# One hybrid decoder layer: another order of the projection blocks, the last y in SBUF, and a second top-k by lookups of two-byte values

## The chip, the cores and the metric

The kernel runs on one core of a Trainium2 chip. The metric is the device time of one execution in microseconds (us). The engines are named as the profile names them: PE (matrix multiplication), PEld (its weight loads), DVE (vector), ACT (activations), POOL (issues gathers and the transfers that accumulate), SP (issues the other transfers). Each runs its own instructions in a fixed order and waits on semaphores for the others.

## The reference

One layer on 512 tokens of width 1024, with 16 learned meta tokens put in front, all in fp32. It has two residual sub-layers and a last RMSNorm:

```
u = rmsnorm(h);  z, xBC, dt, conf = split(u @ w_in)
xBC  = silu(causal depthwise conv of width 4)
y    = chunked scan (chunks of 128, 16 heads, 4 groups), + D * x, * silu(z), rmsnorm per group
hc   = causal depthwise conv of width 31 of a * sigmoid(g)     (a, g = conf)
c    = silu(LayerNorm(hc))
h    = h + concat(y, c) @ w_out

q    = rmsnorm(h) @ w_query                    # 8 heads, two halves
v1,i1 = top16(q1 . keys1);  v2,i2 = top16(q2 . keys2)          # of 128 each
top_s, pos = top16(v1[:, None] + v2[None, :])                  # of 256 sums
expert = i1 * 128 + i2 at pos;  gate = softmax(top_s)
h    = h + sum_k gate_k * gelu(x . w_down[expert_k]) * w_up[expert_k]
out  = rmsnorm(h) without the meta tokens
```

There are 16384 experts, each one row of w_down and one of w_up.

## The kernel before, in words

An fp32 product is made of three matmuls of rounded halves (mm3, L160 to L162): high by high, high by low, low by high. A weight block is loaded raw by SP, rounded by ACT (L181, L182), and its low half is finished by a transfer of POOL that accumulates (L183). Two raw and two split buffers alternate.

Stage 1 (0 to 39 us) normalizes the tokens in five tiles (four of 128 and the 16 meta tokens), transposes them (L280) and splits them into halves (L263, L264). z0, the first projection block, is multiplied after that, tile by tile of tokens, with its split weights (L207) loaded in two halves.

Stage 2 (to about 310 us) runs the other 19 blocks of 96 matmuls. The string ORDER names them: z blocks are the gates of y, x blocks the inputs of the scan with their short convolution (taps L362 to L373 on DVE), c blocks the Conformer's. A c block (L398 on) leaves a and g in PSUM; DVE multiplies them (L406, L407: the GLU) and then makes 30 taps of 128x512 on DVE (L413), with late priority (LOWP). The first c block's sum over its channels is used as an offset for the others (L419, L393). When x4 to x7 and a group's own x and z blocks are done, the group's scan follows (ssd, L505 on): per chunk matmuls, exponentials on ACT, and on DVE L515 to L544. It writes y to DRAM (yD). PSUM has two rings of four tiles, pa and pb.

Stage 3 (to 488 us): y is read back, transposed (L591) and split (L597, L598). The output projection has four blocks of four weight rows (out_part), each with two column halves and its own adds into the residual (L620). The Conformer's LayerNorm takes sums over all channels by matmuls with ones (L643, L644), in PSUM columns that each get two matmuls; the moments are L646 to L653. Its results are transposed rows (L393 again), then L658 to L663. Blocks 0 and 1 belong to y, 2 and 3 to the Conformer. The second RMSNorm follows (L669 to L682, transposes L581).

Stage 4 (488 to 600 us): queries, keys, and the first top-16 of 128 for 4 token tiles, 8 heads and 2 halves (L743 to L747, at L789's scores).

Stage 5 (600 to 1026 us): the second top-16 per token tile, in the order 3, 0, 1, 2 (second, L826 on). Only the pairs that can be among the best 16 sums are built, 50 per head, with their sums (cS) and their expert numbers (cI); the expert number at each of the 16 places is picked by a compare with 50 numbers, a product and a sum over 3200 fp32 elements, for each half of the heads (L836, L838, L839). For tiles 0 to 2 both indices and the gate are transposed (L858) and kept as two-byte values. They become dense gate maps (L916 to L938, 12 of 32 tokens), while PE runs 88 blocks of x @ w_down of 24 matmuls each (down). Tile 3 is done by gathering rows: POOL issues each gather (L873), DVE uses it (L889, L896), through two buffers at first.

Stage 6 (from 1026 us) runs the 128 up blocks with what is left of down and of the gathers, and the last norm.

A scheduler that models the engines sets each engine's order, by priorities and offsets: early(SSDP) for the scan, late(LOWP) for the taps, early(YP) with YP = -500 for the output of y, early(LNP) for the LayerNorm.

Of the kernel before, what the change touches and what calls it, by code (L numbers as in the profile page):

```python
# [43 lines left out]
ORDER = "z0 x4 x5 x6 x7 x0 c0 c1 x1 c2 x2 c3 z1 x3 c4 c5 z2 c6 z3 c7".split()  # L44
# [73 lines left out]
def body(ctx, tc, I, out):  # L118
# [146 lines left out]

    for n, t in enumerate(MO):
# [7 lines left out]
        for half in range(2):  # L274
# [7 lines left out]
            split_to(uTh[:, half * 4:half * 4 + 4, c0:c0 + parts], uTl[:, half * 4:half * 4 + 4, c0:c0 + parts], pv)  # L282

# [23 lines left out]
    yD = dram.tile([4, 128, 1024], F32, name="yD")  # L307


    dtraw = con(80)  # L310

    def z_block(k):
        if k == 0:
            zn = 272
            wh, wl = zsplit
        else:
            zn = 256
            wh, wl = next_w()
        for t in MO if k == 0 else range(4):
            p = ps("pa")  # L320
            c0 = NM + 128 * t if t >= 0 else 0
            z0 = 0 if t >= 0 else 256
            for dc in range(8):
                mm3(p[:, z0:zn], uTh[:, dc, c0:c0 + 128], uTl[:, dc, c0:c0 + 128],
                    wh[:, dc * zn + z0:dc * zn + zn], wl[:, dc * zn + z0:dc * zn + zn], dc == 0, dc == 7)
            if k == 0:
                V.tensor_copy(dtraw[:, 16 * (t + 1):16 * (t + 2)], p[:, 256:272])
            if t < 0:
                continue
            zt = ZB[k % 2][:, t, :]  # L330
            S.activation(zt, p[:, :256], AF.Tanh, scale=0.5)
            V.scalar_tensor_tensor(zt, zt, 1.0, p[:, :256], op0=OP.add, op1=OP.mult)
# [169 lines left out]
    def ssd(g):  # L502
# [4 lines left out]
        for c in range(5):  # L507
# [11 lines left out]
            if c > 0:  # L519
# [18 lines left out]
                y_ = ybs[n % 3]  # L538
# [9 lines left out]
                load(yD[c - 1, :, 256 * g:256 * g + 256], y_)  # L548
# [36 lines left out]
    yh = [mem(B0 + 512 * k, 512) for k in range(4)]  # L585
# [22 lines left out]
    def out_part(b):  # L608
        for hf in range(2):
            po = [ps("pa") for _ in range(4)]  # L610
            src = I["wout"][hf, b].rearrange("p k n -> p (k n)")
            wh, wl = wsplit(wload(src), src)
            for t in range(4):
                for k in range(4):
                    sh, sl = hl((b % 2) * 4 + k)
                    mm3(po[t], sh[:, 128 * t:128 * t + 128], sl[:, 128 * t:128 * t + 128],
                        wh[:, 512 * k:512 * k + 512], wl[:, 512 * k:512 * k + 512], k == 0, k == 3)
            for t in range(4):
                hh = h1[t][:, 512 * hf:512 * hf + 512]
                V.tensor_tensor(hh, hh, po[t], op=OP.add)  # L620

    with early(YP):
        n = 0
        for g in range(2):
            for t in range(4):
                load(yq[n % 4], yD[t, :, 256 * g:256 * g + 256])
                y_split(yq[n % 4], t, g, 1)
                n += 1
        for t in range(4):
            load(h1[t], I["x"][128 * t:128 * t + 128])  # L630
        out_part(0)
        for t in range(4):
            load(yh[t], yD[t, :, 512:1024])
            y_split(yh[t], t, 2, 2)
        out_part(1)


    with early(LNP):
        p = ps()
        for c0, (a_, b_) in ((0, (sumd, convo[:, 7, :])), (4, (sumq, sq7[0]))):  # L640
            for t in range(4):
                ts = slice(128 * t, 128 * t + 128)
# [397 lines left out]
```

## Time and profile before

| what | value |
| --- | --- |
| median of three runs | 1749.32 us (1747.53 to 1750.86) |
| profiled execution | 1744.54 us, span 1742.8 us |
| granted clock of PE, mean | 0.969 |
| PE busy | 1642.9 us, 94% |
| DVE busy | 1446.8 us, 83% |
| ACT busy | 767.2 us, 44% |
| POOL busy | 394.3 us, 23% |

Rows of groups read: line, engine, operation, output <- inputs, shapes, count | busy us, mean ns | idle time of the engine just before, and what ended it. Rows of waits read: who <- whom: us in total, times, longest.

### The profile page before, as it was taken

The numbers are of one execution on the slowest core, as the hardware profiler recorded it, in microseconds if no ns is written. First come the engines' busy times: TensorE is split into PE (matmuls) and PEld (weight loads), VectorE is DVE, ScalarE is ACT, GpSimd is POOL, SyncE is SP. The second block draws the span as 40 slices with busy tenths as digits, with TensorE's granted clock in tenths as the row PEclk, the third lists the DMA queues.
The fourth block names the chain that finished last, engine by engine and source line by source line (L and its number), as shares of the span: only waits on it lengthen the run. The fifth ranks groups of instructions, "written<-read, shape, count | busy, mean of one in ns | idle before, by whom it ended". The sixth has DMA issues, their size and how long they took to land.

```text
span 1742.8 us, 26076 instructions
## 1 busy us (share of the span) xinstructions
PE 1642.9 (94%) x9529; PEld 1485.8 (85%) x9529; DVE 1446.8 (83%) x2873; ACT 767.2 (44%) x1117; POOL 394.3 (23%) x317
## 2 busy tenths in 40 slices
PE   6999999758989999989999999999999999999997
PEld 6999899637778899979988988888888899999996
DVE  4559999995359999999888988888888888888885
ACT  5655555434333334424655873333333333333333
POOL 1001011110000002423333003223222255444540
PEclk9999999867999999989999999999999999999999
DMA  6766567443532346768897789999999999999992
GB/s 207 170 156 155 130 153 186 135 117 82 145 106 73 97 159 232 265 211 284 296 310 288 271 290 375 342 347 364 343 341 366 325 322 364 345 351 342 327 333 81
DMA packets 163025, 426.43 MB, mean 245 GB/s; under 512 B 14144, under 2 KB 80960, under 8 KB 154832
## 3 DMA queue, kind: packets, MB, share of 16 engines
q1 hardware_dynamic: 122144, 262.22, 42.9%
q0 software_dynamic: 40752, 162.55, 30.2%
q8 instruction: 74, 1.21, 0.3%
q14 instruction: 55, 0.45, 0.1%
HBM read 382.24 MB, written 42.47 MB: 244 GB/s over the span
## 4 chain that ended last, share of the span: by engine, by line
PE 74%; DMA 10%; DVE 6%; issue 5%; ACT 3%; POOL 2%; SPq 0%; POOLq 0%; DVEq 0%; ACTq 0%
PE pa L162 16%; PE pa L161 16%; PE pa L160 16%; PE pb L162 6%; PE pb L160 6%; PE pb L161 6%; DMA MR<-win 3%; DVE M L413 3%; DMA M<-wu,M 3%; POOL M L873 1%; DMA MR<-wout 1%; PE pb L932 1%; PE pb L933 1%; DMA M<-wd,M 1%; PE pb L786 1%
## 5 line engine op out<-in xcount | busy, mean ns | idle before, releaser
L161 PE MATMUL pa<-MR 128*128 128x512 f32 (+3 forms) x2120 | 729.0, 344 | 5.1 <-DMA MR<-wout 5.1
L160 PE MATMUL pa<-MR 128*128 128x512 f32 (+3 forms) x2120 | 728.8, 345 | 5.3 <-ACT M L761 2.5
L162 PE MATMUL pa<-MR 128*128 128x512 f32 (+3 forms) x2120 | 690.2, 345 | 10.0 <-DVE MR L739 6.1
L162 PEld LDWEIGHTS pa<-MR 128*128 128x128 f32 x2120 | 402.4, 190 | 43.1 <-DVE MR L739 6.6
L160 PEld LDWEIGHTS pa<-MR 128*128 128x128 f32 x2120 | 404.1, 191 | 37.4 <-ACT M L761 3.4
L161 PEld LDWEIGHTS pa<-MR 128*128 128x128 f32 x2120 | 403.5, 190 | 36.3 <-DMA MR<-wout 6.3
L738 ACT ACTIVATE MR<-M 128x1024 fp32r<-128x1024 f32 (+1 forms) x264 | 286.0, 1084 | 289.9 <-PE pa L161 122.0
L739 DVE TENSOR_TENSOR MR<-M,MR 128x1024 fp32r<-128x1024 f32 (+1 forms) x264 | 329.3, 1250 | 45.2 <-ACT MR L738 44.3
L873 POOL DMA_INDIRECT M<-wd,M x128 | 171.4, 1339 | 491.5 <-DVE M L889 229.3
L873 POOL DMA_INDIRECT M<-wu,M x128 | 173.6, 1356 | 363.7 <-DVE M L896 215.5
L160 PE MATMUL pb<-MR 128*128 128x384 f32 (+1 forms) x576 | 206.9, 359 | 0.0
L161 PE MATMUL pb<-MR 128*128 128x384 f32 (+1 forms) x576 | 206.6, 359 | 0.0
L162 PE MATMUL pb<-MR 128*128 128x384 f32 (+1 forms) x576 | 205.5, 359 | 0.0
L959 ACT ACTIVATE MR<-M 128x384 fp32r<-128x384 f32 x128 | 66.9, 523 | 264.8 <-issue 208.4
L896 DVE SCALAR_TENSOR_TENSOR M<-M 128x1024 f32<-128x1024 f32 x128 | 163.6, 1278 | 17.9 <-DMA M<-wu,M 17.6
L413 DVE SCALAR_TENSOR_TENSOR M<-M 128x512 f32<-128x512 f32 x240 | 170.6, 740 | 2.4 <-ACT M L411 2.2
L889 DVE SCALAR_TENSOR_TENSOR M<-M 128x1024 f32<-128x1024 f32 x128 | 154.4, 1216 | 6.4 <-DMA M<-wd,M 6.3
L960 DVE TENSOR_TENSOR MR<-M,MR 128x384 fp32r<-128x384 f32 x128 | 71.0, 556 | 59.1 <-ACT MR L959 59.1
L161 PEld LDWEIGHTS pb<-MR 128*128 128x128 f32 x576 | 108.1, 188 | 11.4
L160 PEld LDWEIGHTS pb<-MR 128*128 128x128 f32 x576 | 108.1, 188 | 11.3
L935 ACT ACTIVATE M<-pb 128x512 f32<-128x512 f32 x96 | 97.0, 1159 | 46.2 <-PE pb L933 43.5
L162 PEld LDWEIGHTS pb<-MR 128*128 128x128 f32 x576 | 108.1, 188 | 10.4
(217 smaller groups left out, 1521.4 us busy)
## 6 DMA issues: line engine op xcount, KB each, us to landing
M<-wdT SPq DMA_DIRECT2D x128, 512.0 KB, 5.1
M<-wu SPq DMA_DIRECT2D x128, 512.0 KB, 6.7
GD<-M SPq DMA_DIRECT2D x40, 512.0 KB, 6.2
M<-GD SPq DMA_DIRECT2D x32, 640.0 KB, 7.9
M<-win SPq DMA_DIRECT2D x19, 1024.0 KB, 4.8
MR<-win POOLq DMA_DIRECT2D x19, 1024.0 KB, 8.2
HD<-M SPq DMA_DIRECT2D x88, 192.0 KB, 4.0
M<-HD SPq DMA_DIRECT2D x88, 192.0 KB, 6.2
```

The costliest lines, as they stand in the source:

```text
L160: E.matmul(o, lh, rh, start=first, stop=False)
L161: E.matmul(o, lh, rl, start=False, stop=False)
L162: E.matmul(o, ll, rh, start=False, stop=last)
L413: V.scalar_tensor_tensor(o, gl[:, j:j + 512], cw[:, j:j + 1], o, op0=OP.mult, op1=OP.add)
L738: S.activation(wh, raw, AF.Copy)
L739: leng.tensor_tensor(wl, raw, wh.bitcast(F32), op=OP.subtract)
L873: r = G.indirect_dma_start(out=g, out_offset=None, in_=src, in_offset=bass.IndirectOffsetOnAxis(ap=e3[:, k:k + 1], axis=0))
L889: use(V.scalar_tensor_tensor(g, g, 1.0, x2s, op0=OP.mult, op1=OP.mult, accum_out=dots[:, k:k + 1]))
L896: use(V.scalar_tensor_tensor(h1[3], g, act3[:, k:k + 1], h1[3], op0=OP.mult, op1=OP.add))
L935: S.activation(gb.rearrange("p i t -> p t i")[:, c:c + 4, :], p.rearrange("p (t i) -> p t i", t=4), AF.Copy, scale=1.0 / GS)
L959: S.activation(sh, sf, AF.Copy)
L960: V.tensor_tensor(sl, sf, sh.bitcast(F32), op=OP.subtract)
```

## The change

Five things change.

1. ORDER: c0 comes directly behind z0, c1 behind x4, c2 behind x6; c3, c4 and c5 keep places in the middle, c6 and c7 stay last.
2. z0 is multiplied as each token tile is transposed and split (z_tile); its weights are split at the first tile, and the second half of them is loaded before the meta tokens. The norm weight is loaded before the constants.
3. The y of the last group stays in SBUF (YL) and is neither written to DRAM nor read. Group 2 is read alone. Output blocks 2 and 3 accumulate into one PSUM tile, so that each residual half gets one add less.
4. The LayerNorm's sums are 16 matmuls into 16 columns, and a DVE instruction more adds the halves.
5. The second top-k builds 80 candidates in a grid of 10 rows of 8 (three adds), takes the place of each winner, turns it into a place in each of the two lists of 16, and picks the two indices by a lookup of 16 two-byte values each: compare, product, and four adds that halve the row.

The core of the diff:

```diff
-ORDER = "z0 x4 x5 x6 x7 x0 c0 c1 x1 c2 x2 c3 z1 x3 c4 c5 z2 c6 z3 c7".split()
+ORDER = "z0 c0 x4 c1 x5 x6 c2 x7 x0 z1 x1 c3 c4 z2 x2 c5 z3 x3 c6 c7".split()
...
+    def z_tile(k, t, zn, wh, wl):
+        p = ps("pa")
+        c0 = NM + 128 * t if t >= 0 else 0
+        z0 = 0 if t >= 0 else 256
+        for dc in range(8):
+            mm3(p[:, z0:zn], uTh[:, dc, c0:c0 + 128], uTl[:, dc, c0:c0 + 128],
+                wh[:, dc * zn + z0:dc * zn + zn], wl[:, dc * zn + z0:dc * zn + zn], dc == 0, dc == 7)
...
-        if n == 1:
+        if n == 0:
             z_split()
...
+        z_tile(0, t, 272, *zsplit)
...
-                y_ = ybs[n % 3]
+                y_ = ybs[n % 3] if g < 3 else YL[c - 1]
...
-                load(yD[c - 1, :, 256 * g:256 * g + 256], y_)
+                if g < 3:
+                    load(yD[c - 1, :, 256 * g:256 * g + 256], y_)
...
+            todo = [(t, n) for n in range(len(bs)) for t in range(4)]
+            for t, n in todo if hf == 0 else sorted(todo):
+                wh, wl = ws[n]
+                for k in range(4):
+                    sh, sl = hl((bs[n] % 2) * 4 + k)
+                    mm3(po[t], ..., n == 0 and k == 0, n == len(bs) - 1 and k == 3)
+                if n == len(bs) - 1:
+                    hh = h1[t][:, 512 * hf:512 * hf + 512]
+                    V.tensor_tensor(hh, hh, po[t], op=OP.add)
...
+        out_part([0])
+        y_group(2)
         for t in range(4):
-            load(yh[t], yD[t, :, 512:1024])
-            y_split(yh[t], t, 2, 2)
-        out_part(1)
+            y_split(YL[t], t, 3, 1)
+        out_part([1])
...
-        for c0, (a_, b_) in ((0, (sumd, convo[:, 7, :])), (4, (sumq, sq7[0]))):
+        for c0, src in ((0, sumd), (4, sumq), (8, convo[:, 7, :]), (12, sq7[0])):
             for t in range(4):
-                E.matmul(p[:, c0 + t:c0 + t + 1], a_[:, ts], ones[:, 0:1], start=True, stop=False)
-                E.matmul(p[:, c0 + t:c0 + t + 1], b_[:, ts], ones[:, 0:1], start=False, stop=True)
+                E.matmul(p[:, c0 + t:c0 + t + 1], src[:, 128 * t:128 * t + 128], ones[:, 0:1], start=True, stop=True)
...
-    out_part(2)
-    out_part(3)
+    out_part([2, 3])
...
+    def lookup(o, at, values):
+        half = lambda a: a.rearrange("p n (j s) -> p n j s", s=2)
+        io = iota16[:, 0:16].rearrange("p (j s) -> p j s", s=2)[:, None].to_broadcast([128, 128, 8, 2])
+        V.tensor_tensor(half(oneh), io, at[:, :, None, :].to_broadcast([128, 128, 8, 2]), op=OP.is_equal)
+        h4 = lambda a: a.rearrange("p (h k) c -> p h k c", h=8)
+        V.tensor_tensor(h4(picked), h4(oneh), values[:, :, None, :].to_broadcast([128, 8, 16, 16]), op=OP.mult)
+        src = picked
+        for f in fold:
+            n = f.shape[2]
+            V.tensor_tensor(f, src[:, :, 0:n], src[:, :, n:2 * n], op=OP.add)
+            src = f
+        V.tensor_tensor(o[:, :, None], src[:, :, 0:1], src[:, :, 1:2], op=OP.add)
...
-        V.tensor_copy(posf, posu.bitcast(U32))
-        for hf in range(2):
-            hs = slice(4 * hf, 4 * hf + 4)
-            V.tensor_tensor(oneh, iota50..., h16(posf)..., op=OP.is_equal)
-            V.tensor_tensor(oneh, oneh, cI..., op=OP.mult)
-            V.tensor_reduce(h16(ef)[:, hs, :], oneh, axis=AX.X, op=OP.add)
+        V.tensor_scalar(rowi.bitcast(I32), posu.bitcast(I32), 3, None, op0=OP.logical_shift_right)
+        V.tensor_scalar(coli.bitcast(I32), posu.bitcast(I32), 7, None, op0=OP.bitwise_and)
...
+        V.tensor_tensor(ab[0], pair(i1f), pair(tmpf), op=OP.add)
...
+        V.tensor_tensor(ab[1], pair(i2f), pair(tmpf), op=OP.add)
+        lookup(i1f, ab[0], idx16[:, 0])
+        lookup(i2f, ab[1], idx16[:, 1])
```

The lines of the changed kernel are other numbers: GLU L408 and L409, taps L415, x taps L364, statistics matmuls L650, y's transposes L593, moments L652, index transposes L873, a gather's use L904, lookups L825 to L833.

How the change moves instructions is shown at three places. First DVE behind the time-step arithmetic of z0 (L465 to L473 before, L467 to L475 now). Before, the taps of the first x block (L362) come there, and the GLU of the first c block some 25 rows later:

```order
L470 SCALAR_TENSOR_TENSOR M<-M 128x64
L471 SCALAR_TENSOR_TENSOR M<-M 16x16
L473 SCALAR_TENSOR_TENSOR M<-M 128x80
L487 COPY M<-M 128x192
L362 SCALAR_TENSOR_TENSOR M<-M 128x528 x3
L478 TENSOR_SCALAR M<-pb 128x80
```

Now the GLU stands ahead of the last of that arithmetic and the first taps (L415) right behind it:

```order
L408 SCALAR_TENSOR_TENSOR M<-M,pa 128x272
L468 TENSOR_SCALAR M<-M 128x80
L409 SCALAR_TENSOR_TENSOR M<-M,pa 128x256
L469 SCALAR_TENSOR_TENSOR M<-M 128x80
L472 SCALAR_TENSOR_TENSOR M<-M 128x64
L473 SCALAR_TENSOR_TENSOR M<-M 16x16
L475 SCALAR_TENSOR_TENSOR M<-M 128x80
L489 COPY M<-M 128x192
L415 SCALAR_TENSOR_TENSOR M<-M 128x512 x3
```

The first c block's work moved ahead of all x taps.

Second PE at the end of the scan: the last chunk's product (L542, now L544), y's transposes (L591, now L593), the LayerNorm's sums (L643, now L650), and the matmuls of an output block (L160 to L162). Before:

```order
L524 MATMUL pb<-M 128x256
L542 MATMUL pb<-M 128x64 x4
L591 MATMUL pa<-M 128x128 x4
L643 MATMUL pb<-M 128x1
L591 MATMUL pa<-M 128x128 x4
L160 MATMUL pa<-MR 128x512
```

Now:

```order
L526 MATMUL pb<-M 128x256
L544 MATMUL pb<-M 128x64 x4
L650 MATMUL pb<-M 128x1 x16
L593 MATMUL pa<-M 128x128 x2
L593 MATMUL pa<-M 128x128 x2
L160 MATMUL pa<-MR 128x512
```

All 16 sums moved ahead of the last transposes of y; before, 15 of 16 stood behind 17 matmuls of the output block that follows.

Third DVE at the second top-k of a tile. Before, its large steps are the compare, product and sum over 3200 elements (L836, L838, L839), between weight splits (L739) and a gather's use (L889):

```order
L836 TENSOR_TENSOR M<-M 128x3200
L744 MAX_INDEX M<-M 128x8
...
L838 TENSOR_TENSOR M<-M 128x3200
L889 SCALAR_TENSOR_TENSOR M<-M 128x1024
L746 MAX M<-M 128x8
L739 TENSOR_TENSOR MR<-M,MR 128x1024
...
L839 TENSOR_REDUCE M<-M 128x64
```

Now a lookup stands there as compare (L825), product (L827) and halving adds (L831, L833):

```order
L825 TENSOR_TENSOR M<-M 128x2048
L856 TENSOR_TENSOR M<-M 128x256
...
L748 TENSOR_TENSOR MR<-M,MR 128x1024
L827 TENSOR_TENSOR M<-M 128x2048
L904 SCALAR_TENSOR_TENSOR M<-M 128x1024
...
L831 TENSOR_TENSOR M<-M 128x1024
L825 TENSOR_TENSOR M<-M 128x2048
```

Six passes of 3200 elements became four of 2048 with small adds. On PE the transposes of the first dense tile's indices (L858, now L873) moved from behind the 32nd down block to behind the 22nd and 23rd.

More of the change, by code (lines that the diff above doesn't have):

```diff
@@ L306, in body @@
     xws = [mem(W0 + 5376 + 256 * k, 256) for k in range(3)]
-    yD = dram.tile([4, 128, 1024], F32, name="yD")
-    dtraw = con(80)
+    YL = [mem(o, 256) for o in (S0 + 4608, S0 + 4864, F0 + 3728, F0 + 3984)]
+    yD = dram.tile([4, 128, 768], F32, name="yD")
     def z_block(k):
         if k == 0:
[L314 to L332, printed above, removed]
+            return
+        zn = 256
+        wh, wl = next_w()
+        for t in range(4):
+            z_tile(k, t, zn, wh, wl)
     Bt = mem(B0, 2048).rearrange("p (c n) -> p c n", c=4)
@@ L606, in body, with out_part @@
     x2s = mem(XS0, 1024)
-    def out_part(b):
+    def out_part(bs):
         for hf in range(2):
             po = [ps("pa") for _ in range(4)]
-            src = I["wout"][hf, b].rearrange("p k n -> p (k n)")
-            wh, wl = wsplit(wload(src), src)
-            for t in range(4):
[L614 to L628, printed above, removed]
+            ws = []
+            for b in bs:
+                src = I["wout"][hf, b].rearrange("p k n -> p (k n)")
+                ws.append(wsplit(wload(src), src))
+            todo = [(t, n) for n in range(len(bs)) for t in range(4)]
[3 more added lines that the diff above has]
+                    sh, sl = hl((bs[n] % 2) * 4 + k)
+                    mm3(po[t], sh[:, 128 * t:128 * t + 128], sl[:, 128 * t:128 * t + 128],
+                        wh[:, 512 * k:512 * k + 512], wl[:, 512 * k:512 * k + 512],
+                        n == 0 and k == 0, n == len(bs) - 1 and k == 3)
+                if n == len(bs) - 1:
+                    hh = h1[t][:, 512 * hf:512 * hf + 512]
+                    V.tensor_tensor(hh, hh, po[t], op=OP.add)
@@ L709, in body @@
     idxu = v5(rmem(1024).bitcast(U32))
-    idxf = v5(rmem(1024))
-    cS = rmem(400).rearrange("p (h k) -> p h k", h=8)
-    cI = rmem(400).rearrange("p (h k) -> p h k", h=8)
+    cS = rmem(640).rearrange("p (h r c) -> p h r c", h=8, r=10)
+    idx16 = rmem(128).bitcast(F16).rearrange("p (f h k) -> p f h k", f=2, h=8)
     h16 = lambda a: a.rearrange("p (h k) -> p h k", h=8)
-    ts_, posu, posf, gate, ef, ei, i1f, i2f = [rmem(128) for _ in range(8)]
+    ts_, posu, rowi, gate, rowf, colf, i1f, i2f = [rmem(128) for _ in range(8)]
+    spare = rmem(1024)
+    tmpf, coli = [spare[:, 128 * k:128 * k + 128] for k in range(2)]
     GRES = rp[0]
```

73 lines of the change are left out of this document (39 added, 34 removed).

## The prediction

> **What bounds the kernel now.** I read the page first, then the busy time in windows by stage, then the waits, then single lines. The page gives the whole and the two engines that matter:
>
> ```profile
> span 1742.8 us, 26076 instructions
> PE 1642.9 (94%) x9529; PEld 1485.8 (85%) x9529; DVE 1446.8 (83%) x2873; ACT 767.2 (44%) x1117; POOL 394.3 (23%) x317
> ```
>
> The share of PE is an average. Windows by stage (start:end, length, then busy time and count of PE, its weight loads, DVE, ACT, POOL, then granted clock, DMA share, GB/s) split it by what is done:
>
> ```profile
> 0.00:120.00 120.00, 102.70 (x806) 100.81 (x807) 60.23 (x137) 71.45 (x116) 9.80 (x17) 1.00 0.67 179
> 120.00:300.00 180.00, 173.92 (x1391) 168.95 (x1390) 171.03 (x318) 96.75 (x172) 20.02 (x22) 0.98 0.61 155
> 300.00:410.00 110.00, 74.23 (x356) 59.62 (x355) 96.55 (x200) 39.59 (x91) 10.30 (x11) 0.72 0.46 123
> 410.00:488.00 78.00, 69.02 (x301) 55.84 (x300) 39.47 (x65) 37.64 (x48) 5.96 (x8) 0.96 0.47 119
> 488.00:600.00 112.00, 111.39 (x562) 95.77 (x563) 89.18 (x461) 37.65 (x47) 0.55 (x1) 0.98 0.26 90
> 600.00:1000.00 400.00, 381.57 (x2525) 369.20 (x2523) 372.61 (x768) 200.03 (x256) 101.50 (x51) 0.97 0.74 254
> 1000.00:1743.00 743.00, 730.04 (x3600) 635.64 (x3597) 617.73 (x927) 284.10 (x390) 246.11 (x209) 0.99 0.91 327
> ```
>
> Up to 120 us DVE idles for 60 us while PE is mostly busy. From 300 to 410 it is the other way round: DVE is nearly full, PE idles 36 us and its clock falls to 0.72. From 600 to 1000 both are close to full. Behind 1000 PE counts, and nothing in that stage is changed. Single lines tell what fills DVE in the middle (count, shortest/median/longest ns, first and last start):
>
> ```profile
> L407 DVE SCALAR_TENSOR_TENSOR M<-M,pa x8: 401/414/423, 117.3 to 309.3; 128x256 f32<-128x256 f32 x8
> L413 DVE SCALAR_TENSOR_TENSOR M<-M x240: 729/742/753, 120.4 to 395.3; 128x512 f32<-128x512 f32 x120
> L646 DVE TENSOR_SCALAR M<-pb x1: 167/167/167, 408.9 to 408.9; 128x8 f32<-128x8 f32 x1
>   PE pb L644: 4.7, 1
> ```
>
> The GLU (L407) of the first c block runs at 117.3, of the last at 309.3. The 240 convolution taps (L413) fill the time up to 395.3, and the LayerNorm moments (L646) come at 408.9, after 4.7 us in which DVE waits for L644.
>
> **The change part by part.** The order of blocks first. The first c block moves from the seventh place to the second, so taps can start behind z0 and one block, at about 48 us and not at 120.4. In the order of DVE's instructions 74 of the 240 taps stand behind the last GLU before, 55 after. The price of a tap and of its neighbours:
>
> ```profile
> L413 DVE SCALAR_TENSOR_TENSOR M<-M 128x512 f32<-128x512 f32 x240 | 170.6, 740 | 2.4 <-ACT M L411 2.2
> L620 DVE TENSOR_TENSOR M<-M,pa 128x512 f32<-128x512 f32 x32 | 21.6, 681 | 35.6 <-PE pa L162 35.6
> L591 PE MATMUL pa<-M 128*128 128x128 f32 x32 | 8.6, 413 | 21.5 <-DMA M<-yD 21.5
> ```
>
> A tap costs 170.6/240 = 0.71 us, so 19 fewer are 13.5 us. The stretch from last GLU to moments was 408.9 - 309.3 = 99.6 us. Less 13.5 it is 86. Of the rest, the kernel before loses time to y's way through DRAM: PE waits 21.5 us for loads of yD, and L643/L644 stand behind the last of them on PE. The change keeps the y of the last group in SBUF and sets the four half sums as 16 independent matmuls ahead of the last transposes. That removes the 4.7 us of idle DVE and about 3 us of small work behind it: 4 more transposes' splits stand behind the moments. One SSD chunk more (7 for 6) is left behind the last GLU, already counted by its instructions in the 3. So the stretch takes about 79 us (74 to 85).
>
> The last GLU itself waits for PE, which runs the 19 projection blocks nearly without a gap. Before 300 PE loses most at the start, and then from 120 to 300 some 6.1 us of idle and 0.02 x 174 = 3.5 of clock. The one long wait at the start (us in total, times, longest), and the wait of the first convolution's statistics (L393) for DVE:
>
> ```profile
> PE pb L280 <- DVE M L276: 9.6, 1, 9.6
> ...
> L393 PE MATMUL pb<-M 128*128 128x128 f32 x24 | 4.2, 330 | 2.0 <-DVE M L420 2.0
> ```
>
> z0 multiplied token tile by token tile puts 24 matmuls into the 9.6 us in which PE waits for the next normalized tile; before, all z0 work stood behind nearly all transposes. It can save between 0 and 9.6 us. I take 4, since these matmuls also wait for the split weights, whose loads are only reordered. Of the 9.6 us behind 120 I take 4 back: 2.0 is the wait for L420, which will be long done when PE comes there, and some clock with it. The last GLU then comes at 309.3 - 8, say 300 (292 to 306), and the moments at 300 + 79 = 379: **30 us earlier** (18 to 40).
>
> Some is given back. In the order before, 45 matmuls of 512 columns of the second output block ran ahead of the LayerNorm's transposes, now 22; PE does the other 23 later. While nothing but down blocks runs, a matmul of 384 columns takes 0.172 us:
>
> ```profile
> 640.00:680.00 40.00, 40.00 (x232) 40.00 (x231) 40.00 (x100) 17.40 (x23) 3.55 (x2) 1.00 0.59 203
> ```
>
> So one of 512 columns takes about 0.23, and 23 take 5.3 us. The merged last two output blocks save 8 of the 32 adds L620 (0.68 us each) in a stretch where PE, not DVE, is busy; I count 2 us for that and for weights that are fetched a little earlier. **Mixing layer: 30 - 5.3 + 2 = 27 us** (15 to 38).
>
> Then the second top-k. The rows for what goes and for what comes:
>
> ```profile
> L836 DVE TENSOR_TENSOR M<-M 128x3200 f32<-128x3200 f32 x8 | 27.8, 3475 | 0.0
> L927 DVE TENSOR_TENSOR M<-M 128x1024 f16<-128x1024 f16 x96 | 62.0, 684 | 0.6
> L739 DVE TENSOR_TENSOR MR<-M,MR 128x1024 fp32r<-128x1024 f32 x256 | 311.1, 1217 | 40.4 <-ACT MR L738 39.5
> L739 DVE TENSOR_TENSOR MR<-M,MR 128x2048 fp32r<-128x2048 f32 x8 | 18.2, 2275 | 4.8 <-ACT MR L738 4.8
> L743 DVE MAX8 M<-M x96: 182/274/296, 512.7 to 748.1; 128x8 f32<-128x128 f32 x64, 128x8 f32<-128x50 f32 x32
> L817 DVE TENSOR_TENSOR M<-M 128x128 f32<-128x128 f32 x8 | 2.2, 272 | 0.0
> ```
>
> Per token tile six passes over 3200 elements go: 6 x 3.475 = 20.9 us. Two sets of seven small adds (272 ns the largest, 1.4 us a set) become one set of three, 1.1: 1.7 saved. Top-16 over 80 candidates in place of 50: MAX8 takes 182 ns at its shortest (50 values) and 274 in the median (128), so 35 more for 30 values; with five such steps and eight heads 1.4 us more. Index arithmetic: about 1 us more (four more instructions near 0.25). Two lookups come. Two-byte 1024 elements take 684 ns, what fp32 takes for 512 (L620); so 2048 take what fp32 takes for 1024, 1.217. A lookup is 2 x 1.217 + 0.68 + 0.41 + 0.27 + 0.27 = 4.1 us, two are 8.1. Sum: 20.9 + 1.7 - 1.4 - 1.0 - 8.1 = **12 us of DVE per tile, 48 in all**. At fp32's rate a lookup would be 2 x 2.275 + 1.22 + 0.68 + 0.41 + 0.27 = 7.1, the saving 6 per tile. I take the fast rate: the compares of L924/L925 have the same operand form (pairs) as the lookups, and L927's time.
>
> What that is worth is set by PE, which stands nearly full. Its idle time from 600 to 1000 is 18 us, and the clock of 0.97 costs 0.03 x 382 = 11. So at most 29 can be won. How much stays is read from these rows:
>
> ```profile
> L858 PE MATMUL pb<-M x9: 270/271/331, 730.0 to 838.7; 128*128 128x128 f32 x9
>   DVE M L855: 0.2, 1
> DVE M L896 <- DMA M<-wu,M: 17.6, 4, 6.1
> M<-wd,M POOLq DMA_INDIRECT x128, 7.1
> M<-wu,M POOLq DMA_INDIRECT x128, 7.3
> L873 POOL DMA_INDIRECT M<-wu,M x128 | 173.6, 1356 | 363.7 <-DVE M L896 215.5 <-PE pb L933 96.9 <-DVE M L889 40.3
> L896 DVE SCALAR_TENSOR_TENSOR M<-M x128: 1271/1278/1290, 849.9 to 1705.9; 128x1024 f32<-128x1024 f32 x128
> ```
>
> L858 are the transposes of the chosen indices. On PE the first tile's stand behind 32.1 of the 88 down blocks before, behind 23.5 after: 8.6 x 24 x 0.172 = 35.5 us sooner. On DVE the instructions from the first top-16 pass up to them sum to 239 us before and 207 after by the means of their rows; before they took 730.0 - 512.7 = 217, so after 188: 29 sooner. PE waited 0.2 us for DVE there, so there was no slack, and it will now stall 6 us. How stalls weigh is seen in two other places:
>
> ```profile
> 444.40:447.10 2.70, 0.09 (x1) 0.00 (x0) 0.00 (x0) 2.67 (x2) 0.00 (x0) 1.00 0.92 185
> 447.70:451.00 3.30, 3.30 (x9) 2.61 (x8) 0.00 (x0) 0.00 (x0) 0.58 (x1) 0.50 1.06 302
> 484.20:488.60 4.40, 0.02 (x1) 0.02 (x1) 4.40 (x7) 2.78 (x7) 0.00 (x0) 1.00 0.67 238
> 488.60:492.00 3.40, 3.39 (x13) 2.94 (x14) 3.39 (x7) 1.20 (x2) 0.55 (x1) 0.51 0.89 308
> ```
>
> After 4.4 us of idle PE the clock is 0.51 for 3.4 us, which loses 1.7; after 2.6 us the same. So the stall costs 8. The Trainium skill ("TensorE: Matmul & The Clock Gate", section Part 1: The HAM clock gate) lets the clock fall only after an idle window of about 3.4 us; the 2.6 us row disagrees, though the window may have caught the idle pieces before it. By the rule, stalls under 3.4 us would lose no clock and the second half would come out some 2 us better than I sum it.
>
> Gathers are the other limit. 48 of them ran in this stretch through two buffers. A buffer's turn is the gather (7.3), its issue (L873, 1.36) and its use (L896, 1.28), so the ring gives one per 5.0 us. By the sums of rows in the two orders, the DVE work from one use to the next was 5.2 on average and is now 4.4. The ring falls behind: 0 to 48 x 0.6 = 27 us of waits on DVE; I take 8 that reach PE, since PE has down blocks to run. Counting 2 more for smaller stalls that stay, what is left is 29 - 8 - 8 - 2 = **11 us** (0 to 22).
>
> Sum: 27 + 11 = 38. The profiled execution took 1744.54 (span 1742.8 and 1.7 around it), so 1706.5; it lay 4.8 under the median of 1749.32, so on the scale of the median **1711 us**.
>
> **Rivals.**
>
> The gather ring takes the second half. The four waits of L896 (17.6 us) show the ring already late, and its pace of 5.0 is above the new 4.4; against it, PE has 88 blocks that need no gather. Gain 27 + 0 to 3: 1721.
>
> Both engines fit better. With taps from 48 us on, DVE has slack for all but what stands behind the last GLU; if PE reaches that at 292 and the second half gets 20 back, the gain is 38 + 20 = 58: 1691. For it: DVE idles 60 us early. Against: PE left 6 us unused even in its best stretch before 300.
>
> The order does not do what it says, because the chain of SSD chunks and not the taps ends last. The chunks start later, behind five more blocks, and 7 of 16 are behind the last GLU; if one takes what the last six took before, 99.6/6 = 16.6, the seven need 116 us, the moments come at 416 and not at 409. With 11 from the second half, 5 lost behind the moments and 2 saved there, the gain is 1: 1748. Against it: those six chunks shared DVE with 74 taps.
>
> Slower: PE starves during the projections. A c block's PSUM tiles are freed by its GLU on DVE, and each GLU now stands in DVE's order behind up to 34 taps and the taps of x blocks. From the first GLU to the second, third and fourth DVE's rows sum to 21, 56 and 113 us; PE has 2, 5 and 10 blocks until then, and a block is 96 matmuls of the 1391 that filled 174 us: 24, 60 and 120. PE can run one block, 12 us, ahead. If DVE is late by more than that from the third c block on, each of six blocks loses the excess; 7 us each make 42 and eat the 38: 1753. From 120 to 300 DVE was busy 171 of 180 us; at that rate 113 us of work take 119, so DVE arrives with PE and 12 us before it decides.
>
> **How the numbers follow.** Forecast 0.55, with its own range 1702 to 1720; ring 0.20; better fit 0.13; SSD chain 0.06; slower 0.06. The range takes the ends 15 + 0 and 38 + 20: 1691 to 1734. A change of 0.2% (3.5 us) is about what this kernel's measurement can tell from none. Faster: 0.55 + 0.20 + 0.13 + 0.02 of the SSD case = 0.90; same 0.03 and slower 0.01 of it; slower 0.07 in all.
>
> **What would show it.** Right: first tap near 48 us; last GLU near 300, moments near 379, no yD wait at the end; windows from 320 to 380 still full on DVE; six passes of 3.5 us gone, the 2048-element ops at 1.2 us; a PE stall of some 6 us at the first L873 matmul; first up block near 988. Wrong: PE idle between 60 and 200 behind GLUs; moments beyond 395; two-byte ops near 2.3 us; waits on gathers above 40 us before the up stage.

## The result and the profile after

The changed kernel takes 1717.67 us (median of four runs, 1714.89 to 1719.04) where the kernel before takes 1748.88: a ratio of 0.9819, 95% interval 0.9802 to 0.9836, 31 us less. The forecast was 1711 with a range of 1691 to 1734. The profiled executions differ by less, 1742.8 - 1716.4 = 26.4 us of span; their parts are what the text goes by.

Windows of the changed kernel (columns as in the prediction) up to 410 us and from 600 to 1000:

```profile
0.00:120.00 120.00, 103.58 (x815) 101.55 (x816) 86.38 (x175) 66.23 (x100) 10.43 (x16) 1.00 0.67 180
120.00:300.00 180.00, 173.76 (x1372) 167.96 (x1371) 160.17 (x301) 101.65 (x183) 19.45 (x22) 0.97 0.61 151
300.00:410.00 110.00, 92.50 (x454) 74.79 (x453) 97.41 (x208) 52.12 (x110) 11.35 (x12) 0.83 0.47 129
600.00:1000.00 400.00, 386.32 (x2671) 373.18 (x2670) 336.87 (x699) 221.24 (x277) 83.23 (x54) 0.98 0.79 271
```

DVE now works 86 of the first 120 us and not 60. From 300 to 410 PE is busy 92.5 and not 74.2 us. From 600 to 1000 DVE's busy time falls from 373 to 337, but PE's only rises from 382 to 386.

Single lines of the changed kernel: the GLU, the taps, the moments, the transposes ahead of the queries (L584, L581 before), and those of the chosen indices (L873):

```profile
L409 DVE SCALAR_TENSOR_TENSOR M<-M,pa x8: 414/416/422, 48.1 to 307.3; 128x256 f32<-128x256 f32 x8
L415 DVE SCALAR_TENSOR_TENSOR M<-M x240: 729/744/754, 50.5 to 369.2; 128x512 f32<-128x512 f32 x120
L652 DVE TENSOR_SCALAR M<-pb x1: 168/168/168, 384.9 to 384.9; 128x8 f32<-128x8 f32 x1
L584 PE MATMUL pb<-M x32: 270/272/421, 460.7 to 474.6; 128*128 128x128 f32 x32
L873 PE MATMUL pb<-M x9: 271/272/327, 667.4 to 753.7; 128*128 128x128 f32 x9
```

The same transposes ahead of the queries in the kernel before:

```profile
L581 PE MATMUL pb<-M x32: 271/273/431, 482.3 to 495.9; 128*128 128x128 f32 x32
```

So the steps are: last GLU 309.3 to 307.3 (2 us); from there to the moments 99.6 to 77.6 (22 us); from the moments to L584 73.4 to 75.8 (2.4 us lost); from there to the end 1742.8 - 482.3 = 1260.5 to 1255.7 (4.8 us). They sum to 26.4.

What PE waits for up to 300 us, before:

```profile
PE pb L280 <- DVE M L276: 9.6, 1, 9.6
PE pa L280 <- DVE M L276: 4.8, 1, 4.8
PE pa L162 <- DMA MR<-win: 3.9, 6, 1.3
PE pb L419 <- issue: 2.8, 1, 2.8
PE pb L393 <- DVE M L420: 2.0, 1, 2.0
```

and now the longest:

```profile
PE pa L162 <- DMA MR<-win: 9.0, 6, 2.6
PE pb L299 <- DVE M L295: 7.8, 1, 7.8
PE pb L526 <- DVE M L558: 2.0, 1, 2.0
PE pa L161 <- DMA MR<-win: 1.0, 1, 1.0
```

The wait for the first tile became shorter, the one for the second tile (4.8) and those for the first convolution went, and the waits for weight blocks (win) grew from 3.9 to 10.0 us. Behind 300 PE's waits for reads of yD fell from the 21.5 us of the prediction's row to 2.6, and DVE's wait at the moments from 4.7 to 2.4.

From 470 us on to the up stage, PE's longer waits in the changed kernel, and below them DVE's waits for gathers:

```profile
PE pb L947 <- DVE M L942: 7.6, 5, 3.0
PE pa L162 <- DVE MR L748: 5.2, 1, 5.2
PE pb L873 <- DVE M L833: 0.5, 1, 0.5
...
DVE M L904 <- DMA M<-wd,M: 15.5, 11, 3.9
DVE M L911 <- DMA M<-wu,M: 11.7, 5, 5.8
```

The wait for a weight split (L748; 6.1 us before, at L739) and those for gate maps (L942; 8.8 before, at L927) are nearly what they were. The lookups' two large steps:

```profile
L825 DVE TENSOR_TENSOR M<-M 128x2048 f16<-128x2048 f16 x8 | 9.8, 1221 | 0.0
L827 DVE TENSOR_TENSOR M<-M 128x2048 f16<-128x2048 f16 x8 | 9.7, 1215 | 0.0
```

### The profile page after: what moved, and what is told of

Its sections match the earlier page's. It is cut to its first block, busy times and chain, and to the rows that moved or that the text cites. A ratio compares the mean times of both kernels' runs of the same rounds, so it can differ in the third digit from the quotient of the medians.

```text
span 1716.4 us, 26056 instructions
## 1 busy us (share of the span) xinstructions
PE 1641.1 (96%) x9529; PEld 1483.6 (86%) x9529; DVE 1397.5 (81%) x2864; ACT 768.3 (45%) x1117; POOL 376.6 (22%) x317
## 5 line engine op out<-in xcount | busy, mean ns | idle before, releaser
L160 PE MATMUL pa<-MR 128*128 128x512 f32 (+3 forms) x2120 | 728.8, 345 | 5.8 <-ACT M L770 1.7
L162 PE MATMUL pa<-MR 128*128 128x512 f32 (+3 forms) x2120 | 692.0, 345 | 15.3 <-DMA MR<-win 9.0
L162 PEld LDWEIGHTS pa<-MR 128*128 128x128 f32 x2120 | 403.6, 191 | 48.1 <-DMA MR<-win 10.3
L160 PEld LDWEIGHTS pa<-MR 128*128 128x128 f32 x2120 | 404.8, 191 | 38.5 <-ACT M L770 2.3
L747 ACT ACTIVATE MR<-M 128x1024 fp32r<-128x1024 f32 (+1 forms) x264 | 285.8, 1083 | 306.8 <-PE pa L161 127.3
L748 DVE TENSOR_TENSOR MR<-M,MR 128x1024 fp32r<-128x1024 f32 (+1 forms) x264 | 330.1, 1251 | 100.8 <-ACT MR L747 99.9
L888 POOL DMA_INDIRECT M<-wd,M x128 | 156.4, 1222 | 473.4 <-DVE M L904 211.8
L160 PE MATMUL pb<-MR 128*128 128x384 f32 (+1 forms) x576 | 206.6, 359 | 0.0
L162 PE MATMUL pb<-MR 128*128 128x384 f32 (+1 forms) x576 | 205.0, 359 | 0.0
L415 DVE SCALAR_TENSOR_TENSOR M<-M 128x512 f32<-128x512 f32 x240 | 173.3, 743 | 2.2 <-ACT M L413 1.2
L904 DVE SCALAR_TENSOR_TENSOR M<-M 128x1024 f32<-128x1024 f32 x128 | 154.6, 1218 | 15.7 <-DMA M<-wd,M 15.5
L160 PEld LDWEIGHTS pb<-MR 128*128 128x128 f32 x576 | 108.1, 188 | 11.4
L162 PEld LDWEIGHTS pb<-MR 128*128 128x128 f32 x576 | 108.1, 188 | 10.3
```

The lines of the kernel that those rows point to most:

```text
L160: E.matmul(o, lh, rh, start=first, stop=False)
L162: E.matmul(o, ll, rh, start=False, stop=last)
L415: V.scalar_tensor_tensor(o, gl[:, j:j + 512], cw[:, j:j + 1], o, op0=OP.mult, op1=OP.add)
L747: S.activation(wh, raw, AF.Copy)
L748: leng.tensor_tensor(wl, raw, wh.bitcast(F32), op=OP.subtract)
L888: r = G.indirect_dma_start(out=g, out_offset=None, in_=src, in_offset=bass.IndirectOffsetOnAxis(ap=e3[:, k:k + 1], axis=0))
```

## The experiments

### The order of blocks alone

The kernel before, with the new string ORDER.

> The kernel before with the new order of blocks and nothing else. Theory A (the tail behind the last GLU is DVE work, and y's way through DRAM is a second, smaller part of it): 19 taps fewer behind the last GLU, 13.5 us, but the moments still wait behind the last load of yD; the moments come near 395 in place of 409 and the time is 1733 to 1738. Rival B (the load of yD ends the tail whatever stands before it): under 5 us gained, 1744 or more. Rival C (the order is the whole gain of the mixing layer): moments near 385, 1725 to 1729.

1735.22 us beside 1744.29 (ratio 0.9946, 0.9929 to 0.9962). GLU and moments:

```profile
L407 DVE SCALAR_TENSOR_TENSOR M<-M,pa x8: 403/418/423, 50.5 to 311.5; 128x256 f32<-128x256 f32 x8
L646 DVE TENSOR_SCALAR M<-pb x1: 168/168/168, 394.3 to 394.3; 128x8 f32<-128x8 f32 x1
```

Theory A: the moments come at 394.3, 14.6 us earlier. The stretch behind the last GLU shrinks by 16.8 us (99.6 to 82.8), a little more than the 13.5 of the 19 taps. The last GLU itself comes 2.2 us later than before, in one execution of each: starting the taps early does not help PE, and its waits for weight blocks up to 300 us are already 7.5 us in place of 3.9.

### The second top-k of before

The changed kernel with second(), its buffers and its tables as before (six passes over 3200 elements in place of the lookups).

> The changed kernel with the second top-k of before (50 candidates, six passes over 3200 fp32 elements a tile). Theory A (PE is nearly full in this stage, so most of the 48 us of DVE was not on the path): 3 to 8 us slower than the changed kernel, 1721 to 1726, with about 48 us more DVE busy time from 600 to 1000. Rival B (DVE sets the end of this stage): 20 us slower or more, 1738 and up. Rival C (nothing of it was on the path): 1716 to 1719.

1722.18 us, ratio to the kernel before 0.9877 (0.9861 to 0.9894); the changed kernel has 0.9819, and run again 0.9846 (below). So the lookups are worth 5 to 10 us by these ratios; by the profiles, from L584 to the end, 1261.1 against 1255.7, 5.4. One execution differs from another there by nearly as much: five runs with the same instructions in the same order from L584 on (the changed kernel, the same again, z0 whole, two taps fewer, no transfer) take 1254.4 to 1259.6, the three with the old top-k (before, order alone, this one) 1260.5 to 1264.0. The window from 600 to 1000:

```profile
600.00:1000.00 400.00, 379.45 (x2589) 366.39 (x2588) 370.13 (x663) 210.49 (x265) 104.04 (x51) 0.98 0.76 264
```

DVE is busy 370 and not 337 us there, and 1442.4 and not 1397.5 over the whole span, 44.9 more. Theory A: of some 45 us of DVE work, about 5 were on the path.

### y through DRAM, output blocks and sums as before

```diff
-                y_ = ybs[n % 3] if g < 3 else YL[c - 1]
+                y_ = ybs[n % 3]
-    out_part([2, 3])
+    out_part(2)
+    out_part(3)
```

with out_part, the reads of y and the LayerNorm's paired sums as before.

> The changed kernel with y of all groups written to DRAM and read back, output blocks 2 and 3 apart, and the LayerNorm sums in pairs, as before. Theory A (of 22 us that the stretch from last GLU to moments became shorter, 13.5 are taps and about 8 the yD round trip): moments near 393, 1724 to 1729. Rival B (the order alone shortened the tail): moments near 385, 1716 to 1719. Rival C (what is won here is given back by PE behind the moments): moments near 393 but 1717 to 1721.

1722.09 us, ratio 0.9869 (0.9836 to 0.9901). Last GLU, moments, and transposes ahead of the queries:

```profile
L408 DVE SCALAR_TENSOR_TENSOR M<-M,pa x8: 404/415/423, 49.0 to 307.2; 128x256 f32<-128x256 f32 x8
L647 DVE TENSOR_SCALAR M<-pb x1: 167/167/167, 387.8 to 387.8; 128x8 f32<-128x8 f32 x1
L582 PE MATMUL pb<-M x32: 270/273/446, 468.0 to 482.6; 128*128 128x128 f32 x32
```

The moments come 2.9 us later than in the changed kernel (4.3 later than in its other execution, below) and the transposes 7.3: more of this part's worth lies behind the moments than ahead of them, the other way round from what I had put. From L582 to the end this run takes 1719.7 - 468.0 = 1251.7, 4 us less than the changed kernel with the same code there; its instructions stand in another order there, and this hides half of the 7.3 in the total. None of the three as it stands: the moments are nearer to B (385) than to A and C (393), the time lies just under A.

### z0 as one block

The changed kernel with z_tile called for all tiles behind the loop over them.

> The changed kernel with z0 multiplied as one block behind all tiles of tokens, loads in the changed order. Theory A (what z0 by tile wins at the start is capped by the first weight block, for which PE waits 2.6 us in the changed kernel): 2 to 4 us slower, 1720 to 1722. Rival B (the whole wait of 9.6 us was filled): 8 to 10 us slower, 1726 to 1728. Rival C (DVE sets the end of the mixing layer, so PE's start does not matter): 1716 to 1719.

1723.05 us, ratio 0.9869 (0.9847 to 0.9891), 5 us above the changed kernel. The last GLU comes at 310.7, 3.4 later, the moments 7.5 later:

```profile
L653 DVE TENSOR_SCALAR M<-pb x1: 168/168/168, 392.4 to 392.4; 128x8 f32<-128x8 f32 x1
```

Against the four other executions of the changed projections (next section) the last GLU is 4.0 to 7.0 later. So z0 by tiles is worth 3.4 to 7 us at the last GLU: A, at the upper end of its 2 to 4 us or above. In the tail DVE's instructions stand in another order here, and the stretch from last GLU to moments takes 81.6 us; the 4 us more were not expected.

This run also separates the parts of the change at the start. PE's first wait is 7.7 us here, and 9.5 in the run with the new order alone: the changed loads shorten it, not z_tile. The wait for the second tile, 4.8 us before, is 5.6 here and gone in the changed kernel: z_tile fills that one.

### The changed kernel again, beside three with work on POOL

> The changed kernel as it is, beside the three that follow. Both theories: 0.982 of the time before, 1710 to 1716 where the kernel before takes 1744.

1718.38 us, ratio 0.9846 (0.9811 to 0.9881). In this execution the last GLU came at 305.9 and the moments at 383.5. Three other runs have the same code up to the moments: with the old top-k the last GLU came at 306.7, with the down blocks on POOL at 303.7, with half the gathers at 303.9. So one execution differs from another by up to 3.6 us at this mark. The waits for weight blocks were 7.0 to 8.9 us in these four, and the stretch to the moments 77.6 to 79.1.

The weight blocks' low halves subtracted on POOL:

```diff
-        S.activation(wl, wh.bitcast(F32), AF.Copy, scale=-1.0)
-        G.dma_start(wl, src, accum_op=OP.add)
+        G.tensor_tensor(wl, raw, wh.bitcast(F32), op=OP.subtract)
```

> The changed kernel, but the low half of each projection and output weight block is one subtraction on POOL (128x2048) in place of an ACT pass (1.9 us) and an accumulating transfer (0.9 us to issue, 8.2 to land). Theory A (PE's waits for weight blocks, 9.0 us before 300 in the changed kernel against 3.9 before, are why the last GLU came only 2 us earlier): a subtraction of 2 to 6 us makes these waits vanish, the last GLU comes 5 to 9 us earlier (298 to 302), the time falls by 4 to 10 us against the changed kernel. Rival B (DVE, not PE, sets the last GLU): waits vanish, the last GLU stays at 305 or later, time within 3 us. Rival C (POOL's large operations slow DVE's): taps above 0.80 us each, time up by 5 us or more.

1777.29 us, ratio 1.0175 (1.0139 to 1.0212). The POOL subtraction and the taps:

```profile
L182 POOL TENSOR_TENSOR MR<-M,MR 128x2048 fp32r<-128x2048 f32 x27 | 143.9, 5329 | 219.4 <-ACT MR L181 177.8 <-issue 31.0 <-PE pb L525 10.7
L414 DVE SCALAR_TENSOR_TENSOR M<-M x240: 729/737/5182, 53.8 to 430.3; 128x512 f32<-128x512 f32 x120
```

Rival C, by far: a tap takes 1003 ns on average and not 743, and the last GLU comes at 362. The median of 737 shows that most taps are as fast as ever; the longest takes 5182. One subtraction and the tap that meets it (start, length, in us):

```profile
129.49 4.67 POOL L182 TENSOR_TENSOR MR<-M,MR 128x2048 fp32r<-128x2048 f32 x1 [11.18 <-ACT MR L181]
129.56 5.15 DVE L414 SCALAR_TENSOR_TENSOR M<-M 128x512 f32<-128x512 f32 x1
```

The tap ends half a microsecond behind the subtraction. So DVE does not become slower as a whole: an instruction that meets one of POOL's is held. The 209 taps that meet no subtraction take 739 ns on average, the 31 that do 2.8 us. The run says nothing on A and B.

The offset and the running sums on POOL:

```diff
-                V.tensor_tensor(o, o, crow, op=OP.subtract)
+                (G if k < 7 else V).tensor_tensor(o, o, crow, op=OP.subtract)
-                    V.tensor_tensor(sumq, sumq, at, op=OP.add)
-                    V.tensor_tensor(sumd, ..., o, op=OP.add)
+                    G.tensor_tensor(sumq, sumq, at, op=OP.add)
+                    G.tensor_tensor(sumd, ..., o, op=OP.add)
```

> The changed kernel, but for Conformer blocks 1 to 6 the offset's subtraction and the two running sums (18 operations of 128x512, 0.68 us each, 12 us in all) run on POOL and not on DVE. Theory A (DVE's work alone sets the moments): moments 6 to 12 us earlier (373 to 379), time down by 5 to 11 us. Rival B (PE and the scan's chain of chunks set them): moments within 3 us, time within 3 us. Rival C (POOL's operations slow DVE's): taps above 0.80 us, time up.

1717.61 us, ratio 0.984 (0.9803 to 0.9876): no change against the changed kernel. The moments come at 383.2, within 3 us. The taps:

```profile
L415 DVE SCALAR_TENSOR_TENSOR M<-M 128x512 f32<-128x512 f32 x240 | 180.2, 772 | 3.1 <-ACT M L413 1.8
```

The taps got 6.9 us longer in sum (173.3 to 180.2), which takes back more than half of the 12 us; the stretch from last GLU to moments is 78.9 us, no shorter. So it does not tell A from B.

The split of the down blocks on POOL:

```diff
-            down(i, "pa", True, V)
+            down(i, "pa", True, G)
```

> The changed kernel, but the weight split of the 86 down blocks that run ahead is on POOL and not on DVE (1.22 us each). Theory A (PE's remaining waits from 600 to 1000 come from bursts of DVE work in front of a weight split and of a gate map, not from DVE's sum): the wait of 5.2 us for a split goes, DVE's busy time from 600 to 1000 falls by about 105 us, and the stage becomes 5 to 12 us shorter. Rival B (the same waits come back as waits for POOL, whose subtraction and gathers now share a queue): within 4 us, with waits of PE or of ACT for the POOL subtraction in its place. Rival C (POOL is slower than a down block's 4.1 us): 40 us slower or more.

1791.53 us, ratio 1.0263 (1.0227 to 1.0298): rival C in its size, for another reason. The split takes 2.5 us on POOL, less than a block's 4.1; but DVE's instructions are held behind it:

```profile
L748 POOL TENSOR_TENSOR MR<-M,MR 128x1024 fp32r<-128x1024 f32 x86 | 215.1, 2505 | 218.3 <-ACT MR L747 206.1 <-issue 11.6
L831 DVE TENSOR_TENSOR M<-M 128x512 f16<-128x512 f16 x8 | 11.7, 1465 | 0.0
L939 DVE TENSOR_TENSOR M<-M x48: 674/683/5610, 672.2 to 936.0; 128x1024 f16<-128x1024 f16 x48
```

L939, of the gate maps, takes 684 ns on average in the changed kernel and 1283 here; the median is 683 in both and the longest takes 5.6 us. L831 takes 409 ns there. From 600 to 1000 DVE is busy 366 us, 31 more than in the run beside it, with 105 us of splits fewer to do. PE's waits follow: 27.3 us for the chosen indices (L873) and 32.4 for gate maps (L942), where the changed kernel has 0.5 and 7.6.

### Two taps fewer

```diff
-            for j in range(1, 31):
+            for j in range(1, 29):
```

> The changed kernel with the last two of the 30 taps left out in each Conformer block, so the convolution is incomplete: 224 taps, 46 behind the last GLU and not 55. Theory A (DVE's sum from the first tap on sets the moments): 16 x 0.72 = 11.5 us earlier, moments at 371 to 375. Theory B (PE sets the last GLU, and DVE only what stands behind it): 9 x 0.72 = 6.5 us, moments at 376 to 379, last GLU within 2 us of 306. Theory C (the scan's chain of chunks sets the end): moments within 3 us of 384. The time falls by what the moments gain, less up to 3 us.

1712.67 us, 5 to 6 us under the changed kernel:

```profile
L409 DVE SCALAR_TENSOR_TENSOR M<-M,pa x8: 403/417/422, 49.2 to 307.1; 128x256 f32<-128x256 f32 x8
L652 DVE TENSOR_SCALAR M<-pb x1: 168/168/168, 378.3 to 378.3; 128x8 f32<-128x8 f32 x1
```

Theory B: the last GLU stays where it was, and the moments come 5.2 to 6.6 us earlier. The stretch between them is 71.2 us in place of 77.6, 6.4 less, what the 9 taps fewer behind the last GLU make. PE sets the last GLU; DVE's work counts from there on. The chunks of the scan are the same, so their chain does not set the end.

### No accumulating transfer for the projection blocks

```diff
-        return wsplit(raw, src)
+        return wsplit(raw, src, accum=False)     # leaves out G.dma_start(wl, src, accum_op=OP.add)
```

> The changed kernel, but the 19 projection blocks' low halves are left as the negated high halves: the accumulating transfer of POOL (0.9 us to issue, 8 to land) is left out for them, which takes away PE's waits for weight blocks before 300. Theory A (these waits, 9 us, hold the last GLU back): last GLU 5 to 9 us earlier, 297 to 302, and moments earlier by as much. Theory B (DVE holds the last GLU; PE's waits for weights turn into waits for DVE): no wait for weights, last GLU at 304 or later, moments within 3 us of 384.

1702.02 us, ratio 0.9737 (0.9706 to 0.9769), some 16 us under the changed kernel:

```profile
L410 DVE SCALAR_TENSOR_TENSOR M<-M,pa x8: 402/417/423, 45.3 to 292.9; 128x256 f32<-128x256 f32 x8
L653 DVE TENSOR_SCALAR M<-pb x1: 167/167/167, 370.6 to 370.6; 128x8 f32<-128x8 f32 x1
```

Theory A, and more than its size: against the five executions of the changed projections the last GLU comes 11 to 14 us earlier, and so do the moments. With the waits for win gone DVE follows PE; it was PE, and PE's weights, that held the projections.

### Half the gathers ahead of the up stage

```diff
-SPRATE = (4.0, 1.03, 3.33, 0)
+SPRATE = (2.0, 1.31, 3.33, 0)
```

> The changed kernel with two gathers per gate map in place of four (24 and not 48 ahead of the up stage), and 1.31 per up block in place of 1.03. Theory A (waits of DVE on the two-buffer ring of gathers hold gate maps back, and PE with them): PE's 8 us of waits for L942 and the half clock behind them go, the stage ends 5 to 10 us sooner, time 1708 to 1713 where the changed kernel takes 1718. Rival B (what leaves this stage costs the same in the up stage): within 3 us. Rival C (the bursts of the second top-k alone cause the waits): within 3 us, with the waits for L942 still there.

1727.79 us, ratio 0.9895 (0.9873 to 0.9917), 10 us slower than the changed kernel. The window up to 1000 and the first part of the up stage:

```profile
600.00:1000.00 400.00, 393.89 (x2739) 382.02 (x2738) 312.99 (x654) 222.08 (x281) 42.98 (x31) 0.99 0.74 249
1000.00:1360.00 360.00, 341.17 (x1486) 276.91 (x1485) 308.09 (x483) 123.63 (x168) 126.41 (x107) 1.00 0.99 356
```

The same part of the up stage in the changed kernel:

```profile
1000.00:1360.00 360.00, 358.60 (x1599) 298.53 (x1598) 295.76 (x474) 130.32 (x178) 93.39 (x87) 1.00 0.96 342
```

A is right on the mechanism: the waits for L942 are gone, and PE is busy 7.6 us more up to 1000. B is right on the sum, and too mild: in the first part of the up stage the DMA share is 0.99, PE is busy 17 us less in 360, and from 1000 on it waits 10.4 us for the rounding of up weights (L747) and 8.4 for their low halves (L748), none of it in the changed kernel. The gathers cost something wherever they stand, and more in the later stage.

### Weight blocks in halves

```diff
-        S.activation(wh, raw, AF.Copy)
-        S.activation(wl, wh.bitcast(F32), AF.Copy, scale=-1.0)
-        G.dma_start(wl, src, accum_op=OP.add)
+        for c in (slice(0, n // 2), slice(n // 2, n)):
+            S.activation(wh[:, c], raw[:, c], AF.Copy)
+            S.activation(wl[:, c], wh[:, c].bitcast(F32), AF.Copy, scale=-1.0)
+            G.dma_start(wl[:, c], src[:, c], accum_op=OP.add)
```

> The changed kernel with each projection and output weight block prepared in two halves of 1024 columns: round, negate, accumulate the first half, then the second, so that PE can begin a block when its first half has landed. Theory A (the time from a freed weight slot to the landed low half is what PE waits for, as the run without the accumulating transfer suggested): PE's 9 us of waits for win fall to 3 or less, the last GLU comes at 294 to 301, the moments 6 to 12 us earlier (372 to 378), time 1706 to 1712 where the changed kernel takes 1718. Rival B (the halves' transfers land as late as the whole, since they share the 16 engines): waits as before, time within 3 us. Rival C (two issues of 0.9 us a block fill POOL's queue or the extra ACT passes delay the tanh of c blocks): last GLU later than 308, time up.

1705.55 us (1702.58 to 1708.12), ratio to the kernel before 0.9765 (0.9745 to 0.9785). This is the fastest version found, 12 to 13 us under the changed kernel, and it leaves nothing out:

```profile
L410 DVE SCALAR_TENSOR_TENSOR M<-M,pa x8: 410/414/422, 45.8 to 293.1; 128x256 f32<-128x256 f32 x8
L653 DVE TENSOR_SCALAR M<-pb x1: 167/167/167, 373.7 to 373.7; 128x8 f32<-128x8 f32 x1
```

Theory A: the last GLU and the time come a little earlier than it says, the moments inside its range, behind a stretch of 80.6 us. PE's list of waits up to 300 us has no row for win any more; it begins with:

```profile
PE pb L300 <- DVE M L296: 7.6, 1, 7.6
```

## Why the prediction was right or wrong

**The whole.** Faster by 1.8%, inside the range; the gain was put at 38 us and is 31 by the medians, 26 by the profiles. The likeliest case (1711) and the ring rival (1721) lie on both sides of 1717.67. The parts came out smaller than forecast, 21.6 for 27 and 4.8 for 11 by the profiles.

**"The last GLU comes at 300" failed.** It came at 307.3, and at 303.7 to 306.7 in the four other executions of the same projections. It had two terms of 4 us.

The first term, the start, came out near its size (3.4 to 7 us) for a reason that the prediction had wrong. The 9.6 us are PE's wait for its very first instruction, from the start of the span on, when no matmul of z0 can run. The changed loads shortened it to 7.8; z_tile filled another wait, the 4.8 for the second tile. That the size fits is partly luck.

The second term, 4 us back from the 9.6 behind 120, did not come. From 120 to 300 PE now idles 6.2 us and loses 0.03 x 174 = 5.2 of clock, 11.4 and not 9.6. The stalls at L419 and L393 did go, but weight blocks took their place: 3.9 to 10.0 us up to 300 (7.0 to 8.9 in the four other executions), of which the order alone makes 7.5 and the first block, which z_tile brings forward, a wait of 2.6 at 32.2. A block's weights need two ACT passes of 1.9 us, an issue of 0.9 and a transfer of 8.1, together 12.8 us after its slot is free (12.2 to 14.9 block by block in the trace); PE needs 12 for a block. The preparation was as long before (12.0 to 14.9), so other work of PE between the blocks must have covered it; that is argued and not measured. The run without the transfer and the run with halves both take the waits away, and the last GLU goes to 293. I had not listed the 3.9 us, and did not ask what a PE without other stalls runs into next.

Between the profiles of the changed kernel and of the run without the transfer the last GLU moves by 14.4 us. PE idles 22.7 us up to it in one and 13.7 in the other, 9.0 less, and its clock loses 5.1 and 1.7, 3.4 less; 2 us stay open.

**"The stretch takes about 79 us" was right**: 77.6, and 77.6 to 79.1 in the four other executions. Its division was not. The order gave 16.8 us (13.5 predicted), and the parts on y and the sums 3 to 5 there, where I had counted 7.7; of the 4.7 us of idle DVE at the moments 2.4 stayed. Behind the moments these parts gave 4 more, where I had counted 2. The run with fewer taps confirms that taps behind the last GLU cost their full time.

**Given back behind the moments**: 3.3 predicted, 2.4 measured.

**"12 us of DVE per tile" was right**: the two large steps take 1221 and 1215 ns (1217 predicted), MAX8 over 80 values 222 (217), and DVE's busy time over the span is 44.9 us less than with the old top-k, 11 a tile.

**"11 us in the second half" was mis-sized**: 4.8 by the profiles. The stall of 6 us at the first index transposes did not come (0.5 us). DVE reached them 41 us sooner, not 29: 667.4 less 491.4, where the first top-16 pass (L752) starts, is 176 us and not 217. DVE is busy nearly throughout both stretches:

```profile
512.70:730.00 217.30, 215.38 (x1178) 201.20 (x1177) 210.47 (x850) 80.30 (x104) 26.16 (x12) 1.00 0.46 156
491.40:667.40 176.00, 175.08 (x948) 161.17 (x947) 167.53 (x815) 67.36 (x86) 11.71 (x7) 1.00 0.43 140
```

Its work fell by 43 us, where the sums of rows had 32; besides the lookups, 23 weight splits of 1024 elements and 5 uses of gathers stand there now, and 32 and 10 before. The stalls that I let vanish stayed instead: 5.2 us for a weight split, which comes 13.6 us behind the one before it (683.93 to 697.54), with steps of the next tile's top-16 and lookup, gather uses and gate maps in between; and 7.6 for gate maps behind gathers. Shorter steps did not help where the order of DVE puts a burst in front of the one instruction that PE waits for. The first up block was forecast near 988. Its first matmul starts at 1003.8, and at 1040.1 in the kernel before, where the 1026 of the stages is too early.

**The gather ring** was the rival that came nearest: DVE's waits on gathers rose from 23.9 to 27.2 us, well under the 27 more that were the upper bound (48 x 0.6 is 28.8; 27 goes with the unrounded pace). The run with half the gathers shows that PE's gate-map waits hang on them. So the total of this rival came near, and its wait did not.

**The other rivals.** PE was not starved by GLUs: no wait of PE up to 300 us names one (L408, L409). The chain of scan chunks does not end the tail: with two taps fewer the stretch shrank by the taps, the chunks being the same. Seven chunks fit into 77.6 us, 11 each, where I had extended 16.6. The better fit did not come: a last GLU near 292 took a kernel without the waits for weights.

## What to carry to other kernels

When a stall of the bounding engine is removed, list what that engine takes in per unit of work (here a weight block every 12 us against 12.8 us of preparation) before booking the gain; a chain that was just hidden is the next wait. Cutting such a preparation into halves, so that work can start on the first, was worth 12 us here, where two taps fewer behind it were worth 5. And an engine's freed time is only a gain if the instruction that others wait for moves forward in its order.

## What the runs showed of the hardware

While POOL runs an operation with two tensors from SBUF, a DVE instruction that meets it is often held until it ends. With the low halves on POOL, one DVE instruction lasts at least 80% as long as POOL's in 17 of 27 subtractions, and with the down blocks' splits there in 53 of 86. A mean hides this: taps of 128x512 in fp32 go from 743 ns to 1003 on average, but 209 of 240 meet no subtraction and take 739. Of 48 two-byte instructions of 1024 elements (L939), 35 meet no split and take 681 ns, the 13 others 2.9 us on average. POOL itself needed 5.3 us for a subtraction of 2048 fp32 elements, 2.5 for 1024 and 1.5 to 2.0 for 512. The Trainium skill ("GPSIMD Engine Reference", section 1. Specifications) says that the two share their SBUF interfaces and contend where DVE has two SBUF inputs; these runs agree and show how long one waits. I had not expected that 12 us of work moved off a full DVE would bring nothing.

PE's clock can fall to about a half behind a pause of 2 us, and need not. In the changed kernel it stayed full behind 2.6 us of idling and fell behind 1.95:

```profile
29.50:32.30 2.80, 0.20 (x3) 0.06 (x1) 0.69 (x1) 0.04 (x1) 0.00 (x0) 1.00 0.43 88
32.30:39.00 6.70, 6.70 (x54) 6.70 (x55) 1.02 (x4) 2.33 (x3) 0.00 (x0) 1.00 0.00 0
264.10:266.20 2.10, 0.15 (x2) 0.08 (x1) 2.10 (x5) 1.53 (x6) 0.00 (x0) 1.00 1.09 222
266.20:273.00 6.80, 6.10 (x25) 5.38 (x26) 6.80 (x14) 1.14 (x2) 0.98 (x1) 0.51 0.18 46
```

Behind 1.9 us of idling at 127.6 it fell too (0.57 for 4 us). The pause at 264 comes in all five executions of these projections; in the run with the down blocks' split on POOL the clock stayed at 1.00 behind it. So the length of a pause does not decide alone, and no run here shows what does. The 2.6 us row of the prediction was thus no exception, and no rule. The Trainium skill ("TensorE: Matmul & The Clock Gate", section Part 1: The HAM clock gate) lets the clock fall after an idle window of about 3.4 us; the two pauses behind which it fell here are shorter, and the measurement decides.
